# A hybrid decoder step on one core: constants of the mixing made as the norm columns arrive, the silu table loaded behind the squares, the broadcast of the first roots inside the second unit

## The chip, the core and the metric

The kernel runs on one core of a Trainium2 chip. The metric is the device time of one execution in microseconds, the median of three runs. Names of engines: PE is the matrix engine (PEld its weight loads), DVE the vector engine, ACT the scalar engine, POOL the general engine, SP the engine whose queue issues nearly all transfers.

## The reference

One layer of a decoder for 1024 prompt tokens and 8 x 8 sample tokens, all in float32, with D = 1024 and a feed-forward width of 2816:

```
x = x + 0.5 * rms_norm(swiglu(rms_norm(x, g_f1pre),  ffn1_gu, ffn1_down), g_f1post)
z = rms_norm(x, g_mix) @ w_in + b_in            # q, k, v | hq, hf, hi, hg
a = rms_norm(windowed attention with sinks(q, k, v))
f = lb + (1 - lb) * sigmoid(hf)                 # lb = first row of softmax over two rows of logits
o = rms_norm(gated recurrence(hq, f, hi)) * silu(hg)
x = x + rms_norm(concat(a, o) @ w_out, g_mixpost)
x = x + 0.5 * rms_norm(swiglu(rms_norm(x, g_f2pre), ffn2_gu, ffn2_down), g_f2post)
rms_norm(x, g) = x / sqrt(mean(x * x) + 1e-6) * g
swiglu(x, gu, down) = (silu(x @ gu[:, :2816]) * (x @ gu[:, 2816:])) @ down
```

## The kernel before

The 1088 tokens are three groups: group 0 has 256 prompt tokens and the 64 sample tokens (320 columns), groups 1 and 2 have 384 each. Every float32 product is made of three fp32r products (`mm3`, lines 258 to 260): an operand is split into a rounded high part, made by ACT (line 235 for a weight tile, 575 for the first tokens), and a remainder, made by DVE (lines 236 and 576); PE adds high x high, high x low and low x high in one bank of PSUM. Four banks of the tag `mm` go round, four of the tag `ax` serve small things.

The first feed-forward layer comes first. For group 0 it runs column block by column block of 128: a gate chain of 24 products (8 slices of D, three products each) and an up chain of 24. The first block is made in `pre_first`, where x comes in, is multiplied by the norm's gain (line 575) and used without the norm's root; the root is a factor of each token, so it is put in later, by a product with `rbs`, the roots spread over all partitions (line 664), after which come silu (665), the product with the up chain (668) and the store. To make `rbs`: ACT squares x (611), DVE adds the squares (613 to 615), PE sums over partitions (`st`, 623), DVE adds epsilon (625), POOL takes the power -1/2 (229), DVE puts the roots on a diagonal (`dg`, 630), PE multiplies it by ones (`rb`, 632), and DVE copies the result out (633).

The next blocks of group 0 are made by `up0`, with two halves of a chain between ticks; a tick lets a background stream go a step further. The stream here is the norm of group 1, then of group 2 (`pre_x` and `bcast_steps`, lines 294 to 324: squares on ACT into `ss` and `sq`, DVE's adds, `st`, `sm`, POOL's power, `dg`, `rb`), whose x is loaded by `load_x` (line 532). Weight tiles of 512 KB come over SP into three buffers (`raw`, line 242); a tile's buffer is free when DVE has made the remainder.

The order within an engine is set by a scheduler at build time, from the order of the code, its own estimates, and `issue_after`, which puts an instruction behind another one of the same engine. `queued` and `do` in `pre_first` make such chains for ACT, DVE and PE. Each engine then runs its list in order, and waits at the head of it.

The constants: `mix_consts` makes masks and, from two rows of logits in `cols`, `lb` and 1 - `lb` (with an Exp on ACT); `gains` halves two gains of norms. Both are called in the block loop of the first layer, as extra work at given blocks, but the scheduler places them.

Of the kernel before, what the change touches and what calls it, by code (L numbers as in the profile page):

```python
# [8 lines left out]
F32 = mybir.dt.float32  # L9
# [35 lines left out]
def tile_step(ctx: ExitStack, tc: tile.TileContext, A: dict, O: dict):  # L45
# [123 lines left out]
    def gains():  # L169
        V.tensor_scalar(halfpost[:, 0:8], cols[:, C_F1POST:C_F1POST + 8], 0.5, None, op0=ALU.mult)  # L170
        V.tensor_scalar(halfpost[:, 8:16], cols[:, C_F2POST:C_F2POST + 8], 0.5, None, op0=ALU.mult)

    def mix_consts():
# [41 lines left out]

        e = cp.tile([P, 3, 4], F32, name="lbe")
        l0, l1 = cols[:, C_LB:C_LB + 4], cols[:, C_LB + 4:C_LB + 8]
        V.tensor_tensor(e[:, 2], l0, l1, op=ALU.max)
        V.tensor_tensor(e[:, 0], l0, e[:, 2], op=ALU.subtract)
        V.tensor_tensor(e[:, 1], l1, e[:, 2], op=ALU.subtract)  # L220
        S.activation(e[:, 0:2], e[:, 0:2], AF.Exp)
        V.tensor_tensor(e[:, 2], e[:, 0], e[:, 1], op=ALU.add)
        V.reciprocal(e[:, 2], e[:, 2])
        V.tensor_tensor(lb, e[:, 0], e[:, 2], op=ALU.mult)
        V.tensor_scalar(omlb, lb, -1.0, 1.0, op0=ALU.mult, op1=ALU.add)

# [308 lines left out]
    def pre_first(wgu, h, wts):  # L535
# [58 lines left out]
        do("ACT", lambda: S.activation(junk[:, :P], ones, AF.Square))  # L594
# [14 lines left out]
        for hf in range(2):  # L609
            x = y[hf][:, :, :w]  # L610
            do("ACT", lambda: S.activation(x, x, AF.Square, scale=RMS))
        sq = [t[:, :, :w] for t in y]
# [18 lines left out]
        bank = axbank("rb")  # L631
        PE.matmul(bank[:, :w], ones, dg[:, :w], start=True, stop=True)
        do("DVE", lambda: V.tensor_copy(rbs, bank[:, :w]))
        return out, queued, last["PE"]
# [8 lines left out]
    def make_ffn(wgu, wdn, h, tag):  # L643
# [28 lines left out]
        def up0(j, wts, after=None):  # L672
            w = WIDTH[0]
            g, u = mmbank(), mmbank()
            for bank in (g, u):
                wt = wts.next()
                for ks in (range(4), range(4, 8)):
                    with tc.issue_after(after) if after is not None else nullcontext():
                        r = proj(bank[:, :w], wt, h[0], w, ks)
                    after = after and r.ins  # L680
                    tick()
                if bank is g:
                    rest = gated0(j, g)
            rest(u)
# [315 lines left out]
        f.begin_pair, f.pair, f.gated0 = begin_pair, pair, both0  # L1000
# [539 lines left out]
    banks, queued, tail = pre_first(A["ffn1_w_gu"], h, w0)  # L1540
    f1.rb = rbs
    with queued("ACT"), queued("DVE"):
        f1.gated0(first[0], banks)
        w0.fill()
# [33 lines left out]
    with tc.tile_pool(name="f1", bufs=1) as tp:  # L1578
        f1.pool = tp
        with tc.issue_after(f1.stored.ins):  # L1580
            xs[1] = load_x(1)
        with queued("ACT"), queued("DVE"):
            f1.up0(first[1], w0, tail)

        def norms():
            for n in (1, 2):
                yield from pre_x(n, xs[n], f1pre, part, f1)

        stream("p1", norms(), 1.1)
        for i, j in enumerate(first[2:]):  # L1590
            if i == 1:
                with tc.issue_after(f1.stored.ins):
                    xs[2] = load_x(2)
            f1.up0(j, w0)
        f1.begin(units(HEAD1))
        need("p1")
        f1.up({2: later(gains), 6: later(mix_consts), 8: misc, NJ - 1: f1.begin_down})
        f1.down(last=lambda: f1.begin_pair(PA, True))
        done1(0)
        f1.pair(PA)  # L1600
# [169 lines left out]
```

## Time and profile before

| what | value |
|---|---|
| median of three runs | 1966.09 us (1965.5 to 1967.4) |
| profiled execution: its time | 1964.23 us |
| profiled execution: its span | 1962.5 us |
| PE busy | 1944.9 us (99%) |
| DVE busy | 1368.5 us (70%) |
| ACT busy | 932.2 us (48%) |
| granted clock of PE, mean | 0.999 |

The span is from the first to the last instruction. In rows of a timeline the first number is the start in us from the span's start, the second the duration, then engine, line, operation, tiles, shape and count (xN: merged rows); a bracket at the end is the time that the engine stood idle before it, and what ended that. Matmuls are pipelined, so a row of PE is longer than its distance to the next one.

### The profile page before, as it was taken

The page shows a single profiled execution, that of the slowest core. Times are in us where ns is not written, and L with a number is a line of the kernel's source. Part 1 is how long each engine was busy: PE and PEld are TensorE (multiplying, and loading weights), DVE is VectorE, ACT ScalarE, POOL GpSimd, SP SyncE. Part 2 cuts the span into 40 slices and gives each one's busy share as a digit, 9 for nine tenths or more (in the row PEclk, how much of TensorE's full clock was granted, in tenths as well). Part 3 has the DMA queues.
Part 4 walks back from the last instruction along what each step waited for, and adds up shares of the span by engine and source line. Part 5 has one row for each costly group of instructions (what it writes and reads, how often), then busy time and mean ns, then how long its engine had stood idle before and what let it go on. Part 6 is the DMA issues. An engine that isn't in the chain of part 4 may idle for free.

```text
span 1962.5 us, 34190 instructions
## 1 busy us (share of the span) xinstructions
PE 1944.9 (99%) x13469; PEld 1828.4 (93%) x13469; DVE 1368.5 (70%) x2211; ACT 932.2 (48%) x1630; POOL 209.1 (11%) x213
## 2 busy tenths in 40 slices
PE   9999999999999999999999999999999999999998
PEld 8999999999998987788899898999999999999887
DVE  6976667777558666866667666745987877655666
ACT  6543333444455544744444565655544444444453
POOL 0000000000004012111232224001000000000202
PEclk9999999999999999999999999999999999999999
DMA  7543345556767645764434343556565545677874
GB/s 238 164 151 145 128 170 172 188 185 216 243 215 229 186 130 174 229 207 130 142 116 152 97 126 105 171 167 199 165 208 192 211 171 192 212 236 227 306 262 142
DMA packets 160396, 358.20 MB, mean 183 GB/s; under 512 B 16284, under 2 KB 59996, under 8 KB 160220
## 3 DMA queue, kind: packets, MB, share of 16 engines
q1 hardware_dynamic: 159228, 354.19, 54.5%
q8 instruction: 105, 1.72, 0.4%
q10 hardware_dynamic: 1008, 1.84, 0.3%
q14 instruction: 55, 0.45, 0.1%
HBM read 279.33 MB, written 77.63 MB: 182 GB/s over the span
## 4 chain that ended last, share of the span: by engine, by line
PE 94%; DVE 2%; DMA 2%; ACT 1%; issue 1%; POOL 0%; SPq 0%; DVEq 0%; POOLq 0%; ACTq 0%
PE mm L258 28%; PE mm L260 28%; PE mm L259 28%; DMA ar<-fa 1%; PE c L260 1%; PE c L258 1%; PE c L259 1%; PE sc L1154 1%; PE pv L1195 1%; PE lv L1228 1%; PE pT L1180 1%; DVE w L236 0%; PE mm L551 0%; PE av L1329 0%; DMA big<-in_x1T_dram 0%
## 5 line engine op out<-in xcount | busy, mean ns | idle before, releaser
L258 PE MATMUL mm<-h,wsph 128*128 128x320 f32 (+1 forms) x1296 | 416.3, 322 | 2.6 <-DVE sg L664 2.6
L259 PE MATMUL mm<-h,wsph 128*128 128x320 f32 (+1 forms) x1296 | 410.3, 317 | 0.0
L260 PE MATMUL mm<-h,wspl 128*128 128x320 f32 (+1 forms) x1296 | 408.9, 317 | 0.0
L236 DVE TENSOR_TENSOR wspl<-raw,wsph 128x1024 fp32r<-128x1024 f32 x200 | 250.7, 1254 | 148.9 <-ACT wsph L235 143.6
L235 ACT CAST wsph<-raw 128x1024 fp32r<-128x1024 f32 x200 | 208.9, 1047 | 296.0 <-PE mm L259 239.8
L235 ACT CAST w<-raw 128x512 fp32r<-128x512 f32 (+1 forms) x226 | 169.5, 754 | 239.7 <-PE mm L259 112.6
L236 DVE TENSOR_TENSOR w<-raw,w 128x512 fp32r<-128x512 f32 (+1 forms) x226 | 196.9, 875 | 85.4 <-ACT w L235 85.3
L258 PEld LDWEIGHTS mm<-h,wsph 128*128 128x128 f32 x1296 | 243.8, 188 | 10.2 <-issue 7.8
L259 PEld LDWEIGHTS mm<-h,wsph 128*128 128x128 f32 x1296 | 244.0, 188 | 1.7 <-issue 0.8
L260 PEld LDWEIGHTS mm<-h,wspl 128*128 128x128 f32 x1296 | 243.6, 188 | 1.4 <-issue 1.0
L258 PE MATMUL mm<-h,w 128*128 128x384 f32 x704 | 235.6, 335 | 0.0
L259 PE MATMUL mm<-h,w 128*128 128x384 f32 x704 | 235.6, 335 | 0.0
L260 PE MATMUL mm<-h,w 128*128 128x384 f32 x704 | 230.6, 335 | 0.0
L258 PE MATMUL mm<-w,h 128*128 128x512 f32 x462 | 181.5, 396 | 1.8 <-DVE big L940 1.3
L259 PE MATMUL mm<-w,h 128*128 128x512 f32 x462 | 180.3, 391 | 0.0
L260 PE MATMUL mm<-w,h 128*128 128x512 f32 x462 | 178.9, 391 | 0.4 <-DVE h L236 0.4
L229 POOL TENSOR_TENSOR sm<-sm,mhalf 128x3 f32<-128x3 f32 (+4 forms) x37 | 36.4, 987 | 1193.5 <-DVE sm L313 501.7
L258 PEld LDWEIGHTS mm<-h,w 128*128 128x128 f32 x704 | 132.2, 188 | 0.2 <-ACT big L754 0.2
L259 PEld LDWEIGHTS mm<-h,w 128*128 128x128 f32 x704 | 132.1, 188 | 0.0
L260 PEld LDWEIGHTS mm<-h,w 128*128 128x128 f32 x704 | 131.7, 188 | 0.0
L235 ACT CAST w<-t 128x512 fp32r<-128x512 f32 x176 | 106.8, 621 | 49.2 <-PE mm L260 46.0
L236 DVE TENSOR_TENSOR w<-t,w 128x512 fp32r<-128x512 f32 x176 | 119.0, 687 | 10.4 <-ACT w L235 10.4
(343 smaller groups left out, 3691.6 us busy)
## 6 DMA issues: line engine op xcount, KB each, us to landing
raw<-in_ffn_w_gu_dram SPq DMA_DIRECT2D x154, 512.0 KB
raw<-in_ffn_w_down_dram SPq DMA_DIRECT2D x74, 512.0 KB
raw<-in_w_in_dram SPq DMA_DIRECT2D x54, 512.0 KB
ar<-fa SPq DMA_DIRECT2D x70, 384.0 KB
big<-in_ffn_w_down_dram SPq DMA_DIRECT2D x88, 256.0 KB
fb<-big SPq DMA_DIRECT2D x44, 512.0 KB
raw<-fb SPq DMA_DIRECT2D x40, 512.0 KB
fa<-big SPq DMA_DIRECT2D x22, 768.0 KB
```

The lines of the kernel that those rows point to most:

```text
L229: G.tensor_tensor(y, x, mhalf[:y.shape[0], :y.shape[1]], op=ALU.pow)
L235: S.copy(hi, src)
L236: return (lo_eng or V).tensor_tensor(lo, src, hi.bitcast(F32), op=ALU.subtract)
L258: PE.matmul(out, a[0], b[0], start=first, stop=False, skip_group_check=resume)
L259: PE.matmul(out, a[0], b[1], start=False, stop=False, skip_group_check=resume)
L260: return PE.matmul(out, a[1], b[0], start=False, stop=last, skip_group_check=resume)
L1154: PE.matmul(banks[g][:, i * 256:i * 256 + wk], zq[64 * g:64 * g + 64, 2 * pr + i, b * P:(b + 1) * P], kx[64 * g:64 * g + 64, k0:k0 + wk], ...
L1180: PE.transpose(bank[:, (i * nk + kb) * P:(i * nk + kb + 1) * P], pt[g][:, i, kb * P:(kb + 1) * P], ident)
L1195: PE.matmul(ob[q0:q0 + 64, c:c + 64], pT[g][:, k1:k1 + 64], vn[:, vb, g * 64:g * 64 + 64], start=kb == 0, stop=kb == nk - 1)
L1228: PE.matmul(b4[ps_, j, a], x[:, a, cs], y[:, a, cs], start=True, stop=True)
```

## The change

Four things are edited. The halved gains and `lb`, `omlb` are made at the start of `pre_first`, in place of a Square on ones that had only loaded a table; the subtractions of the maximum are one instruction instead of two. Behind the two squares of x stands a Silu on ones. The matmul `rb` of the first roots, its copy to `rbs` and the gating of block A are put into a function `spread`, which `up0` calls in block B before the last slice of the up chain; block B's own gating follows its up chain. And `load_x(1)` is called after block B, no longer held behind the store of block A.

```diff
--- before.py
+++ after.py
@@ -166,10 +166,6 @@
     lb = cp.tile([P, 4], F32, name="lb")
     omlb = cp.tile([P, 4], F32, name="omlb")
 
-    def gains():
-        V.tensor_scalar(halfpost[:, 0:8], cols[:, C_F1POST:C_F1POST + 8], 0.5, None, op0=ALU.mult)
-        V.tensor_scalar(halfpost[:, 8:16], cols[:, C_F2POST:C_F2POST + 8], 0.5, None, op0=ALU.mult)
-
     def mix_consts():
         nc.sync.dma_start(sinkb, A["attn_sinks"].partition_broadcast(P))
         snk = cp.tile([4, 2], F32, name="snk")
@@ -212,18 +208,6 @@
         bank = axbank()
         PE.matmul(bank[:, 0:2], tf[:4, 7], snk, start=True, stop=True)
         V.tensor_copy(ssink, bank[:, 0:2])
-
-        e = cp.tile([P, 3, 4], F32, name="lbe")
-        l0, l1 = cols[:, C_LB:C_LB + 4], cols[:, C_LB + 4:C_LB + 8]
-        V.tensor_tensor(e[:, 2], l0, l1, op=ALU.max)
-        V.tensor_tensor(e[:, 0], l0, e[:, 2], op=ALU.subtract)
-        V.tensor_tensor(e[:, 1], l1, e[:, 2], op=ALU.subtract)
-        S.activation(e[:, 0:2], e[:, 0:2], AF.Exp)
-        V.tensor_tensor(e[:, 2], e[:, 0], e[:, 1], op=ALU.add)
-        V.reciprocal(e[:, 2], e[:, 2])
-        V.tensor_tensor(lb, e[:, 0], e[:, 2], op=ALU.mult)
-        V.tensor_scalar(omlb, lb, -1.0, 1.0, op0=ALU.mult, op1=ALU.add)
-
 
     def root(y, x):
         G.tensor_tensor(y, x, mhalf[:y.shape[0], :y.shape[1]], op=ALU.pow)
@@ -591,7 +575,18 @@
             evict(d + 2), evict(d + 3)
             weight(1, hf)
 
-        do("ACT", lambda: S.activation(junk[:, :P], ones, AF.Square))
+        e = cp.tile([P, 3, 4], F32, name="lbe")
+        l0, l1 = cols[:, C_LB:C_LB + 4], cols[:, C_LB + 4:C_LB + 8]
+        do("DVE", lambda: V.tensor_tensor(e[:, 2], l0, l1, op=ALU.max))
+        do("DVE", lambda: V.tensor_tensor(e[:, 0:2], cols[:, C_LB:C_LB + 8].rearrange("p (i a) -> p i a", i=2),
+                                          e[:, 2].unsqueeze(1).to_broadcast([P, 2, 4]), op=ALU.subtract))
+        do("ACT", lambda: S.activation(e[:, 0:2], e[:, 0:2], AF.Exp))
+        for i, c in ((0, C_F1POST), (1, C_F2POST)):
+            do("DVE", lambda: V.tensor_scalar(halfpost[:, 8 * i:8 * i + 8], cols[:, c:c + 8], 0.5, None, op0=ALU.mult))
+        do("DVE", lambda: V.tensor_tensor(e[:, 2], e[:, 0], e[:, 1], op=ALU.add))
+        do("DVE", lambda: V.reciprocal(e[:, 2], e[:, 2]))
+        do("DVE", lambda: V.tensor_tensor(lb, e[:, 0], e[:, 2], op=ALU.mult))
+        do("DVE", lambda: V.tensor_scalar(omlb, lb, -1.0, 1.0, op0=ALU.mult, op1=ALU.add))
         busy(WARM)
         operands(0)
         for i in range(2):
@@ -609,6 +604,7 @@
         for hf in range(2):
             x = y[hf][:, :, :w]
             do("ACT", lambda: S.activation(x, x, AF.Square, scale=RMS))
+        do("ACT", lambda: S.activation(junk[:, :P], ones, AF.Silu))
         sq = [t[:, :, :w] for t in y]
         do("DVE", lambda: V.tensor_tensor(sq[0], sq[0], sq[1], op=ALU.add))
         do("DVE", lambda: V.tensor_tensor(sq[0][:, :2], sq[0][:, :2], sq[0][:, 2:], op=ALU.add))
@@ -628,10 +624,18 @@
         for i in range(3):
             r = rows_of(0, i)
             do("DVE", lambda: V.tensor_scalar(dg[:, i * P:i * P + r], ident[:, :r], sm[:, 1, i:i + 1], None, op0=ALU.mult))
-        bank = axbank("rb")
-        PE.matmul(bank[:, :w], ones, dg[:, :w], start=True, stop=True)
-        do("DVE", lambda: V.tensor_copy(rbs, bank[:, :w]))
-        return out, queued, last["PE"]
+
+        def spread(after):
+            bank = axbank("rb")
+            with tc.issue_after(after):
+                r = PE.matmul(bank[:, :w], ones, dg[:, :w], start=True, stop=True)
+            do("DVE", lambda: V.tensor_copy(rbs, bank[:, :w]))
+            f1.rb = rbs
+            with queued("ACT"), queued("DVE"):
+                f1.gated0(first[0], out[0])(out[1])
+            return r.ins
+
+        return queued, spread, last["PE"]
 
     CHAIN = {1: ("X", True, False), 6: ("X", False, False), 7: ("X", False, False), 4: ("X", False, True),
              5: ("Y", True, False), 3: ("Y", False, True), 2: ("Z", True, True)}
@@ -669,18 +673,23 @@
                 f.stored = nc.sync.dma_start(acts[:, j], t[:, :w])
             return rest
 
-        def up0(j, wts, after=None):
+        def up0(j, wts, after=None, mid=None):
             w = WIDTH[0]
             g, u = mmbank(), mmbank()
             for bank in (g, u):
                 wt = wts.next()
-                for ks in (range(4), range(4, 8)):
+                parts = (range(4), range(4, 8)) if mid is None or bank is g else (range(4), range(4, 7), range(7, 8))
+                for ks in parts:
                     with tc.issue_after(after) if after is not None else nullcontext():
                         r = proj(bank[:, :w], wt, h[0], w, ks)
                     after = after and r.ins
+                    if len(ks) == 3:
+                        after = mid(after)
                     tick()
-                if bank is g:
+                if bank is g and mid is None:
                     rest = gated0(j, g)
+            if mid is not None:
+                rest = gated0(j, g)
             rest(u)
 
         def both0(j, banks):
@@ -997,7 +1006,7 @@
 
         f.head = head
         f.loads0, f.up0, f.begin, f.up, f.begin_down, f.down = loads0, up0, begin, up, begin_down, down
-        f.begin_pair, f.pair, f.gated0 = begin_pair, pair, both0
+        f.begin_pair, f.pair, f.gated0 = begin_pair, pair, gated0
         return f
 
 
@@ -1537,10 +1546,8 @@
     w0 = f1.loads0(first)
     del w0.loads[:2]
     part = {}
-    banks, queued, tail = pre_first(A["ffn1_w_gu"], h, w0)
-    f1.rb = rbs
+    queued, spread, tail = pre_first(A["ffn1_w_gu"], h, w0)
     with queued("ACT"), queued("DVE"):
-        f1.gated0(first[0], banks)
         w0.fill()
     xs = {}
 
@@ -1577,10 +1584,9 @@
 
     with tc.tile_pool(name="f1", bufs=1) as tp:
         f1.pool = tp
-        with tc.issue_after(f1.stored.ins):
-            xs[1] = load_x(1)
         with queued("ACT"), queued("DVE"):
-            f1.up0(first[1], w0, tail)
+            f1.up0(first[1], w0, tail, spread)
+        xs[1] = load_x(1)
 
         def norms():
             for n in (1, 2):
@@ -1594,7 +1600,7 @@
             f1.up0(j, w0)
         f1.begin(units(HEAD1))
         need("p1")
-        f1.up({2: later(gains), 6: later(mix_consts), 8: misc, NJ - 1: f1.begin_down})
+        f1.up({6: later(mix_consts), 8: misc, NJ - 1: f1.begin_down})
         f1.down(last=lambda: f1.begin_pair(PA, True))
         done1(0)
         f1.pair(PA)
```

What the scheduler makes of it follows, at the places that matter. Numbers behind tile names tell instances apart and differ between the two kernels; lines of the kernel after are about 16 lower than those of before for the same code, 4 higher inside `up0` and its gating.

DVE in the first microseconds behind the diagonal of the first roots. Before, from the gains to the next remainder (`sg_255` and `sg_307` are blocks A and B, `mm_125` and `mm_126` block A's gate and up banks; the copy to `rbs` and one `wspl` stand just ahead):

```order
L170 TENSOR_SCALAR halfpost<-cols 128x8
L171 TENSOR_SCALAR halfpost<-cols 128x8
L179 MEMSET amask 128x256
L218 TENSOR_TENSOR lbe<-cols 128x4
L664 TENSOR_TENSOR sg_255<-mm_125,rbs 128x320
L664 TENSOR_TENSOR sg_307<-mm_275,rbs 128x320
L236 TENSOR_TENSOR wspl_280<-raw_277,wsph_279 128x1024
L219 TENSOR_TENSOR lbe<-cols,lbe 128x4
L220 TENSOR_TENSOR lbe<-cols,lbe 128x4
L236 TENSOR_TENSOR wspl_313<-raw_310,wsph_312 128x1024
L668 TENSOR_TENSOR sg_255<-sg_255,mm_126 128x320
L668 TENSOR_TENSOR sg_307<-sg_307,mm_276 128x320
```

And in the change, from the second remainder behind the diagonal on (`sg_333` is block A):

```order
L220 TENSOR_TENSOR wspl_276<-raw_273,wsph_275 128x1024
L632 COPY rbs<-rb_330 128x320
L175 MEMSET amask 128x256
L220 TENSOR_TENSOR wspl_306<-raw_303,wsph_305 128x1024
L668 TENSOR_TENSOR sg_333<-mm_125,rbs 128x320
L668 TENSOR_TENSOR sg_341<-mm_271,rbs 128x320
L282 TENSOR_TENSOR ss_372<-ss_372,sq_374 128x384
L282 TENSOR_TENSOR ss_372<-ss_372,sq_377 128x384
L282 TENSOR_TENSOR ss_372<-ss_372,sq_380 128x384
L220 TENSOR_TENSOR wspl_357<-raw_354,wsph_356 128x1024
L282 TENSOR_TENSOR ss_372<-ss_372,sq_395 128x384
L672 TENSOR_TENSOR sg_333<-sg_333,mm_126 128x320
```

The copy, which stood directly behind the diagonal, now has two remainders ahead of it; a third stands ahead of the first gating, and four adds of the next norm and a remainder ahead of block A's second product.

SP at the start. Before:

```order
L242 DMA raw_260<-in_ffn_w_gu_dram 128x1024
L174 DMA sinkb<-in_attn_sinks_dram 128x8
L176 DMA snk<-in_attn_sinks_dram 4x2x1
L242 DMA raw_277<-in_ffn_w_gu_dram 128x1024
L242 DMA raw_310<-in_ffn_w_gu_dram 128x1024
L242 DMA raw_344<-in_ffn_w_gu_dram 128x1024
L242 DMA raw_397<-in_ffn_w_gu_dram 128x1024
L242 DMA raw_451<-in_ffn_w_gu_dram 128x1024
L669 DMA act_100<-sg_255 128x320
L532 DMA big_269<-in_x1T_dram 128x768 x2
L532 DMA big_270<-in_x1T_dram 128x768 x2
```

And in the change:

```order
L226 DMA raw_262<-in_ffn_w_gu_dram 128x1024
L516 DMA big_346<-in_x1T_dram 128x768 x2
L516 DMA big_347<-in_x1T_dram 128x768 x2
L170 DMA sinkb<-in_attn_sinks_dram 128x8
L172 DMA snk<-in_attn_sinks_dram 4x2x1
L226 DMA raw_273<-in_ffn_w_gu_dram 128x1024
L226 DMA raw_303<-in_ffn_w_gu_dram 128x1024
L226 DMA raw_354<-in_ffn_w_gu_dram 128x1024
```

The four loads of x of group 1 moved from behind the store of block A to the place right behind the third weight tile. On ACT their squares moved ahead with them: six stand in a row behind the cast of `raw_303`, then the cast of `raw_354`, then block A's silu.

PE at the norm of group 2. Before, at the end of an up chain (`mm_776`):

```order
L259 MATMUL mm_776<-h_124,wsph_695 128x320
L260 MATMUL mm_776<-h_122,wspl_696 128x320
L310 MATMUL st_711<-omean,ss_633 128x1 x3
L324 MATMUL rb_755<-dg_718,ones 128x384
L258 MATMUL mm_853<-h_121,wsph_739 128x320
```

In the change, one chain earlier (`mm_785` is that block's gate chain, `mm_786` its up chain; `rb` keeps its place behind the up chain, 26 products after these rows):

```order
L242 MATMUL mm_785<-h_122,wsph_659 128x320
L294 MATMUL st_721<-omean,ss_643 128x1 x3
L243 MATMUL mm_785<-h_124,wsph_659 128x320
L244 MATMUL mm_785<-h_122,wspl_660 128x320
L242 MATMUL mm_786<-h_121,wsph_705 128x320
```

The sums, which stood directly ahead of the broadcast that needs their roots, stand 26 products ahead of it. In the norm of group 1 the sums now stand in block D's gate chain behind 16 products, and the broadcast 33 products later. From some 800 of PE's 10,636 rows on, the order is that of before.

## The prediction

> **What bounds the kernel now.** The page's chain of waits comes first, then the waits of PE over the whole run, then the first 75 us of each engine's timeline, since the scheduled order differs only early in the program.
>
> ```profile
> PE 94%; DVE 2%; DMA 2%; ACT 1%; issue 1%; POOL 0%; SPq 0%; DVEq 0%; POOLq 0%; ACTq 0%
> ```
>
> The kernel ends when PE has done its products; another engine counts only where PE stands still. PE's own timeline has three such places in the stretch that the change touches (a bracket is the idle time just before the row, with what ended it):
>
> ```profile
> 23.34 0.70 PE L632 MATMUL rb<-dg,ones 128*128 128x320 f32 x2
> 26.67 0.38 PE L258 MATMUL mm<-h,wsph 128*128 128x320 f32 x1 [2.64 <-DVE sg L664]
> ...
> 30.27 0.31 PE L258 MATMUL mm<-h,wsph 128*128 128x320 f32 x1
> ...
> 45.39 0.83 PE L310 MATMUL st<-omean,ss 128*128 128x1 f32 x6 [0.90 <-DVE ss L298]
> ...
> 74.58 0.91 PE L324 MATMUL rb<-dg,ones 128*128 128x384 f32 x2 [2.27 <-DVE dg L320]
> ```
>
> I call the column blocks A (made in pre_first), B (the first call of up0), C and D. At 26.67 block C's gate chain needs the bank that holds block A's gate sums, and DVE frees it only by the product with the roots (sg, L664). At 30.27 block C's second chain starts without a wait. At 45.39 and 74.58 PE waits for the sums and the roots of the two other norms. Together that is 2.64 + 0.90 + 2.27 = 5.81 us: nearly all that the change can win.
>
> **The first stall: it stays.** DVE's rows of before give the lengths:
>
> ```profile
> 21.38 0.65 DVE L630 TENSOR_SCALAR dg<-ident,sm 128x128 f32<-128x128 f32 x3 [1.05 <-POOL sm L229]
> 24.07 0.49 DVE L633 COPY rbs<-rb 128x320 f32<-128x320 f32 x1 [2.04 <-PE rb L632]
> 24.48 1.22 DVE L236 TENSOR_TENSOR wspl<-raw,wsph 128x1024 fp32r<-128x1024 f32 x1
> ...
> 25.84 0.27 DVE L179 MEMSET amask<- 128x256 f32 x1
> 26.03 0.10 DVE L218 TENSOR_TENSOR lbe<-cols 128x4 f32<-128x4 f32 x1
> 26.05 0.88 DVE L664 TENSOR_TENSOR sg<-mm,rbs 128x320 f32<-128x320 f32 x2
> 26.84 1.29 DVE L236 TENSOR_TENSOR wspl<-raw,wsph 128x1024 fp32r<-128x1024 f32 x1
> ...
> 28.20 1.21 DVE L236 TENSOR_TENSOR wspl<-raw,wsph 128x1024 fp32r<-128x1024 f32 x1
> 29.34 0.87 DVE L668 TENSOR_TENSOR sg<-sg,mm 128x320 f32<-128x320 f32 x2
> ...
> 40.65 1.21 DVE L298 TENSOR_TENSOR ss<-ss,sq 128x384 f32<-128x384 f32 x2
> ...
> 73.85 0.67 DVE L320 TENSOR_SCALAR dg<-ident,sm 128x128 f32<-128x128 f32 x3
> 74.44 0.88 DVE L664 TENSOR_TENSOR sg<-mm,rbs 128x320 f32<-128x320 f32 x2
> ```
>
> The rb matmul now stands three products earlier, at (30.27 - 26.67) / 24 = 0.15 us each (a chain has 24) 0.45 us. Its copy could start at 24.07 - 0.45 = 23.62. But the order of DVE now has two weight remainders (wspl) between dg and that copy, and a third ahead of sg, where before one stood ahead of sg. Distances between starts: three dg 0.59 (73.85 to 74.44), a wspl 1.14 (28.20 to 29.34), the copy 0.41 (24.07 to 24.48), the memset 0.19 (25.84 to 26.03), a sg pair 0.79 (26.05 to 26.84), and from the start of sg to PE's resumption 0.62 (26.05 to 26.67). So: 21.38 + 0.59 + 2 x 1.14 = 24.25 for the copy, + 0.41 + 0.19 + 1.14 = 25.99 for sg, + 0.62 = 26.61 for PE. That is 0.06 us earlier than 26.67. What the two halfpost gains and the lbe steps gave up on DVE, the extra remainders take back.
>
> **The third remainder and a new wait.** Are its inputs there? ACT's timeline:
>
> ```profile
> 4.07 1.28 ACT L594 ACT_TABLE_LOAD   x1 [4.07 <-DMA cols<-in_cols_dram]
> ...
> 14.34 1.27 ACT L611 ACTIVATE big<-big 128x1280 f32<-128x1280 f32 x1
> 15.52 1.99 ACT L235 CAST wsph<-raw 128x1024 fp32r<-128x1024 f32 x2
> 19.28 1.05 ACT L235 CAST wsph<-raw 128x1024 fp32r<-128x1024 f32 x1 [1.78 <-DMA raw<-in_ffn_w_gu_dram]
> 23.23 1.04 ACT L235 CAST wsph<-raw 128x1024 fp32r<-128x1024 f32 x1 [2.90 <-DMA raw<-in_ffn_w_gu_dram]
> 24.29 1.28 ACT L665 ACT_TABLE_LOAD   x1
> 26.56 0.87 ACT L665 ACTIVATE sg<-sg 128x320 f32<-128x320 f32 x2 [0.99 <-DVE sg L664]
> 27.45 1.28 ACT L221 ACT_TABLE_LOAD   x1
> 28.74 0.21 ACT L221 ACTIVATE lbe<-lbe 128x8 f32<-128x8 f32 x1
> ...
> 36.56 1.57 ACT L297 ACTIVATE sq<-big 128x384 f32<-128x384 f32 x3
> ```
>
> The fifth weight tile lands at 23.23 and its cast ends at 24.27, before 24.25 + 0.60 = 24.85, where DVE wants it: 0.58 us of slack. Behind sg DVE now does three ss adds (the next norm's squares, because its input is loaded earlier), a wspl, an ss add, and only then the second product of block A (sg times mm, L668 of before), which frees the bank of block C's second chain. 25.99 + 0.79 = 26.78; three adds at 0.60 (half of 1.21) make 28.58; the wspl 29.72; one add 30.32; + 0.62 gives PE at 30.94. PE arrives at 26.61 + 3.60 = 30.21. So a wait of **0.73 us** opens where there was none. On ACT the six squares take at most 24.27 + 6 x 0.52 = 27.4, and the cast behind them ends at 28.4, 0.2 us ahead of DVE's need at 28.58. Its tile can be issued when the third remainder ends (21.97 + 1.22 = 23.19) and lands some 3.5 us later (15.72 to 19.28 in the rows below): 26.7, in time. Bounds of the new wait: 0 if the adds run on without gaps and the arrival slips, 1.7 if that tile lands a microsecond later than so reckoned.
>
> **The input of the second token group, moved ahead on SP.**
>
> ```profile
> 8.31 0.43 SPq L174 DMA_DIRECT2D sinkb<-in_attn_sinks_dram  x1
> ...
> 15.72 14.05 SPq L242 DMA_DIRECT2D raw<-in_ffn_w_gu_dram  x5
> 29.84 0.41 SPq L669 DMA_DIRECT2D act<-sg  x1
> 30.30 2.31 SPq L532 DMA_DIRECT2D big<-in_x1T_dram  x4
> ```
> ```profile
> GB/s 265 259 337 345 390 365 369 366 372 367 395 385 399 408 420 423 420 437 417 432 387 417 432 417 387 417 417 359 286 141 76 2 0 0 60 0 0 0 0 0
> ```
>
> The second fence is the transfer rate over 5 to 16 us in 40 slices of 0.275 us: about 400 GB/s until 12.7 us, then nothing. The four x1T loads (4 x 384 KB = 1.57 MB, 3.9 us at 0.4 MB/us) now stand right behind the first three weight tiles, so they fall into that hole: 12.7 + 3.9 = 16.6. They are moved past the sink loads, which nothing early reads, and past six weight tiles. The fourth tile leaves at 15.72, when a raw buffer is freed, and its bytes come after the hole's end or share its last 0.9 us; its remainder has slack (cast ended 20.3, DVE wants it at 23.11). I take nothing for it; the bound is in the rivals.
>
> **The two norm waits: they go.** With x1T issued some 21 us sooner (30.30 before, about 9 now), the st matmuls stand in block D's gate chain after 16 products (they stood a block later). PE is there at 30.94 + 3.60 + 16 x 0.15 = 36.9. DVE's last ss add comes after the second products (30.32 + 0.79), two adds, a sg, a wspl and that add: 31.11 + 1.2 + 0.4 + 1.14 + 0.6 = 34.45, and the cast that this wspl needs is done by 31.3 (PE has read the weights that it overwrites at 30.2, + 1.05). That leaves over 2 us, so the 0.90 goes. The rb of that norm is 33 products later, 4.85 us, against this chain:
>
> ```profile
> 46.62 1.89 POOL L229 TENSOR_TENSOR sm<-sm,mhalf 128x3 f32<-128x3 f32 x1 [19.57 <-DVE sm L313]
> 72.34 0.16 DVE L313 TENSOR_SCALAR sm<-st 128x3 f32<-128x3 f32 x1 [1.78 <-PE st L310]
> 72.58 0.85 POOL L229 TENSOR_TENSOR sm<-sm,mhalf 128x3 f32<-128x3 f32 x1 [24.07 <-DVE sm L307]
> ```
>
> From st to the end of dg takes the 2.27 us that PE waited at 74.58, or 2.27 + 1.04 = 3.3 with the slow power of 1.89. In the second norm st and rb stood next to each other; now 26 products, 3.8 us, lie between them. That covers 3.3, so the 2.27 goes too.
>
> **The start and the table loads.** Exp takes the place of the first Square behind the same load at 4.07, so no load is added there. Its operands need cols, which had landed by 4.07; DVE's five following small steps at 0.2 each:
>
> ```profile
> 6.58 1.01 DVE L576 SCALAR_TENSOR_TENSOR h<-big,cols,h 128x320 fp32r<-128x320 f32 x2 [5.49 <-ACT h L575]
> 31.63 0.17 DVE L223 RECIPROCAL lbe<-lbe 128x4 f32<-128x4 f32 x1
> 31.83 0.16 DVE L224 TENSOR_TENSOR lb<-lbe 128x4 f32<-128x4 f32 x1
> ```
>
> Exp ends near 4.07 + 1.30 + 0.21 = 5.58, four dependent steps at 0.20 end at 6.4, and DVE idles until 6.58: hidden, at worst 0.2 us if not. The silu load goes behind the squares: ACT 14.34 + 1.27 = 15.61, + 1.28 + 0.31 = 17.2, then the cast of block B's second weight ends at 18.2 instead of 16.5. PE's order puts that chain at 19.1 by count of products, and its remainder starts only after the squares' sums, at 18.44 before; 0.2 us of slack. The loads at 24.29, 27.45 and the one after them cost PE nothing before (their idle neighbours wait for DVE and DMA), so dropping them wins nothing. [...]
>
> Behind 75 us I see no new stall: where DVE is full,
>
> ```profile
> 80.00:100.00 20.00, 20.00 (x139) 20.00 (x138) 20.00 (x18) 13.19 (x14) 0.00 (x0) 1.00 0.36 103
> ```
>
> (PE, PEld, DVE and ACT busy, in that order) PE was full as well, and DVE's chain starts from the same rb matmul, so both move forward together. If that cover failed, up to the gain itself would be given back.
>
> **Sum** against the profiled execution (span 1962.5, time 1964.23): - 0.06 + 0.73 - 0.90 - 2.27 = **-2.5**, so 1960.0 and 1961.7. The median of the three runs is 1966.09, 1.9 above the profiled one; carried over: 1966.1 - 2.5 = **1963.6**. The likeliest case's own range takes the new wait from 0 to 1.7: 1962.9 to 1964.6, and a microsecond of spread between medians on either side.
>
> **Rivals.**
> 1. *The waits only move.* DVE is late with the ss adds too, and the norm waits stay: -0.06 + 0.73 = +0.7, 1966.8. For it: DVE gains a wspl ahead of every step of this part. Against: the 2 us of slack. 0.14.
> 2. *More goes than counted.* The new wait stays away and the first stall shrinks by 0.7 or more, up to all of it: -3.9 to -5.9, 1962.2 to 1960.2. For it: the first stall is what the moved broadcast stands before. Against: the two remainders ahead of the copy. 0.13.
> 3. *Slower: x1T takes transfer time from the weights.* Place: 8.3 to 16.6 us on the DMA engines. If all of its 3.9 us falls on the fifth tile, sg comes 3.9 - 0.6 = 3.3 later and PE with it: -2.5 + 3.3 = +0.8, 1966.9; if it falls on the first operands, which ACT takes without idle time, 3.9 more: 1970.8. It decides from a delay of 0.58 + 2.5 = 3.1 us on. Against: the rate is at its top until 12.7 whether x1T is queued or not, and the fifth tile's transfer is after 19.66. 0.10. [...]
> [...]
>
> **How the numbers follow.** The forecast has 0.59. A measurement of this kernel tells 0.2%, 3.9 us, from no change. Faster by more than that needs rival 2 (0.13); slower by more needs the upper half of rival 3 and a bad sum in rival 1 (0.08); the rest, 0.79, is within. The range reaches down to nearly all of rival 2, 1960.4, and up through rival 1 to the lower end of rival 3, 1967.0.
>
> **What would show it.** Right: PE's wait near 26.6 for sg is still 2.3 to 2.8 us; a new wait of 0.3 to 1.7 near 30.2 for the second product of block A; no PE wait at either st or rb; x1T issued from 8.3 on and done before 17; no table load between 20 and 45 us. Wrong: a first wait under 2 us (rival 2), tiles four and five landing after 19.5 and 23.5 (rival 3), a cast of block B's second weight after 18.5 (rival 4), st or rb still waited for (rival 1).

## The result and the profile after

| what | before | after |
|---|---|---|
| median of 11 runs each | 1965.0 us (1962.82 to 1967.4) | 1960.77 us (1958.28 to 1963.14) |
| ratio after / before, 95% interval | | 0.9978 (0.997 to 0.9985) |
| profiled execution: time, span | 1964.23, 1962.5 us | 1958.28, 1956.2 us |
| PE busy | 1944.9 us | 1942.2 us |

The kernel is 4.2 us faster, which is 0.22% (interval 0.15 to 0.30%): just over the 0.2% that the prediction reckoned a measurement to tell from no change. The time lies inside the predicted range of 1960.4 to 1967.0, 2.8 us under the predicted 1963.6. (1.1 us of that is the base: the three runs of before that the prediction had stood at 1966.09, the eleven at 1965.0.) The profiled execution of the kernel after is the fastest of its eleven.

PE's waits in the profile after, the largest first (waited for in us, times, longest):

```profile
PE mm L242 <- DVE sg L668: 2.6, 1, 2.6
PE kT L1333 <- DVE h L424: 1.7, 1, 1.7
PE mm L242 <- DVE big L949: 1.3, 2, 0.9
```

The waits of 2.3 us at `rb` and of 0.9 us at `st` are no longer in the list; the first stall heads it as before. PE's own timeline after, at the four places of the prediction:

```profile
26.52 0.38 PE L242 MATMUL mm<-h,wsph 128*128 128x320 f32 x1 [2.56 <-DVE sg L668]
...
30.11 0.31 PE L242 MATMUL mm<-h,wsph 128*128 128x320 f32 x1
...
35.83 0.31 PE L242 MATMUL mm<-h,wsph 128*128 128x320 f32 x1
35.98 0.72 PE L294 MATMUL st<-omean,ss 128*128 128x1 f32 x6
...
36.80 0.31 PE L244 MATMUL mm<-h,wspl 128*128 128x320 f32 x1
...
66.33 0.72 PE L294 MATMUL st<-omean,ss 128*128 128x1 f32 x6
...
70.81 0.81 PE L308 MATMUL rb<-dg,ones 128*128 128x384 f32 x2
...
71.60 0.31 PE L243 MATMUL mm<-h,wsph 128*128 128x320 f32 x1
```

The same places before, as far as the prediction has not shown them:

```profile
44.18 0.31 PE L259 MATMUL mm<-h,wsph 128*128 128x320 f32 x1
...
46.31 0.31 PE L258 MATMUL mm<-h,wsph 128*128 128x320 f32 x1
...
71.58 0.72 PE L310 MATMUL st<-omean,ss 128*128 128x1 f32 x6
...
75.07 0.56 PE L258 MATMUL mm<-h,wsph 128*128 128x320 f32 x1
75.47 0.31 PE L259 MATMUL mm<-h,wsph 128*128 128x320 f32 x1
```

The second product behind the second norm's `rb` is a good mark, since the same products lie ahead of it in both (290 from the end of the first stall on): it starts at 75.47 before and at 71.60 after, **3.87 us earlier**. The pieces:

- first stall: 26.67 to 26.52, -0.15;
- the sums of norm 1, from the product ahead of them to the second one behind: 44.18 to 46.31 is 2.13 us before; 35.83 to 36.80 is 0.97 us after: -1.16;
- norm 2: from `st` to the mark 3.89 us before (71.58 to 75.47); after 5.27 us (66.33 to 71.60), but with 26 products of 0.147 us in between, so 1.45: -2.44;
- these make -3.75; the rest, -0.12, is a hiccup of about 0.1 us near 40.7 us in before.

Two of the three large waits are gone, and the third stayed at its size. The profiled spans differ by 6.3 us, more than these 3.87 and more than the medians' 4.2. Much of the rest is one stretch. Windows of before and then of after (columns: us, then busy time and count of PE, PEld, DVE, ACT, POOL; then granted clock, DMA share, GB/s):

```profile
900.00:910.00 10.00, 10.00 (x62) 7.41 (x62) 4.78 (x9) 3.44 (x3) 0.00 (x0) 0.83 0.34 108
```
```profile
900.00:910.00 10.00, 10.00 (x90) 8.67 (x89) 7.55 (x16) 7.88 (x9) 2.53 (x2) 1.00 0.49 141
```

In before the granted clock is 0.83 there against 1.00 after, worth about 1.7 us (an estimate: 10 us x 0.17). It is no property of before: a later profile of the unchanged new kernel has 0.88 in that window.

```profile
900.00:910.00 10.00, 10.00 (x82) 8.66 (x82) 6.15 (x12) 5.64 (x5) 2.01 (x2) 0.88 0.53 156
```

### The profile page after: what moved, and what is told of

Same layout as the page of the kernel before. It is cut to its first block, busy times and chain, and to the rows that moved or that the text cites. A ratio compares the mean times of both kernels' runs of the same rounds, so it can differ in the third digit from the quotient of the medians.

```text
span 1956.2 us, 34187 instructions
## 1 busy us (share of the span) xinstructions
PE 1942.2 (99%) x13469; PEld 1826.3 (93%) x13469; DVE 1368.3 (70%) x2210; ACT 930.1 (48%) x1628; POOL 208.1 (11%) x213
## 4 chain that ended last, share of the span: by engine, by line
PE 95%; DMA 2%; DVE 2%; ACT 1%; issue 0%; POOL 0%; SPq 0%; DVEq 0%; POOLq 0%; ACTq 0%
PE mm L242 28%; PE mm L244 28%; PE mm L243 28%; DMA ar<-fa 1%; PE c L244 1%; PE c L242 1%; PE c L243 1%; PE sc L1163 1%; PE pv L1204 1%; PE lv L1237 1%; PE pT L1189 1%; DVE w L220 0%; PE av L1338 0%; PE su L1460 0%; PE av L1341 0%
```

## The experiments

The times are medians beside a kernel before of 1965.1 or 1965.0 us. "The mark" is the second product behind the second norm's `rb`: 75.47 before, 71.60 after. (The expectations call it the first product behind; their numbers are for this row.) In the diffs `...` marks lines left out.

**The early load alone**, on the kernel before:

```diff
-        with tc.issue_after(f1.stored.ins):
-            xs[1] = load_x(1)
         with queued("ACT"), queued("DVE"):
             f1.up0(first[1], w0, tail)
+        xs[1] = load_x(1)
```

> The kernel before with one edit: the loads of x of group 1 called after block B and no longer held. In its order the sums of the first norm stand 34 products ahead of their broadcast (before: 26), those of the second norm 6 products ahead (before: 0, in the change 26). Theory (the early load is what the change won by, the moved broadcast won nothing at the first stall): PE's wait of 0.90 at the first st goes and costs 1.2 less, the wait at the second rb shrinks from 2.27 by 6 x 0.15 = 0.9 to about 1.4, the first stall stays at 2.6; PE's first product behind the second rb at 75.5 - 2.1 = 73.4 us, time about 2 us under before. Rival (the broadcast inside block B is what made room): 75.2 to 75.7 us and no change.

Measured: 1961.49 us, ratio 0.9982 (0.9973 to 0.9992). PE:

```profile
26.52 0.61 PE L258 MATMUL mm<-h,wsph 128*128 128x320 f32 x1 [2.64 <-DVE sg L664]
26.92 0.47 PE L259 MATMUL mm<-h,wsph 128*128 128x320 f32 x1
...
41.25 0.72 PE L310 MATMUL st<-omean,ss 128*128 128x1 f32 x6
...
73.48 0.91 PE L324 MATMUL rb<-dg,ones 128*128 128x384 f32 x2 [1.05 <-DVE dg L320]
```

The wait at the first `st` is gone, that at the second `rb` is down from 2.27 to 1.05, and the mark comes at 74.38 instead of the expected 73.4. What is lost there is not a wait: behind the first stall, products start 0.27 us apart instead of 0.147, some eleven times, which costs about 1.4 us. That half clock (granted 0.50 over 26.5 to 29.7 us) is taken up below; without it the mark would be near 73.0. So one edit of the four has some 2.5 of the 3.9 us at the mark, and 3.6 of the 4.2 us of the medians (about 2 was expected; the interval spans 1.6 to 5.3 us).

**The changed kernel with that load held back** behind the store of block A:

```diff
...
-        xs[1] = load_x(1)
+        with tc.issue_after(f1.stored_a.ins):
+            xs[1] = load_x(1)
```

> The changed kernel with one edit: the loads of x of group 1 held behind the store of block A, as before. In its order st and rb of the second norm stand next to each other again. Theory: both norm waits are back (about 0.9 and 2.3), the first stall is 2.5 to 2.6, PE's first product behind the second rb at 75.2 to 75.4, time within 0.5 us of before. Rival: at least 2 of the 3.9 us stay, 73.5 or earlier.

Measured: 1966.53 us, ratio 1.001 (1.0 to 1.0019); that is 1.4 us above before, where at most 0.5 was expected. The waits are back, the one at `st` at half its size:

```profile
43.89 0.83 PE L294 MATMUL st<-omean,ss 128*128 128x1 f32 x6 [0.41 <-DVE ss L282]
...
73.82 1.65 PE L308 MATMUL rb<-dg,ones 128*128 128x384 f32 x2 [2.27 <-DVE dg L304]
...
75.53 0.47 PE L243 MATMUL mm<-h,wsph 128*128 128x320 f32 x1
```

The mark is at 75.53, as in before (expected 75.2 to 75.4). Part of that is half clock (granted 0.55 over 74.5 to 77 us): from `rb` to the mark it takes 1.71 us here and 0.89 in before. At full clock the mark would be near 74.7, so without the early load the three other edits win at most 0.8 us in the trace, and nothing in the median.

**The constants alone**, on the kernel before: `gains` and the `lbe` steps moved to the start of `pre_first`, as in the change.

> The kernel before with only the constants (halved gains, lb, omlb) made at the start in place of the Square. Theory: DVE's gating of block A comes 0.25 earlier, first stall 2.4, both norm waits as before (0.9 and 2.3), PE's first product behind the second rb at 75.1 to 75.4, time within 0.5 us of before. Rival (the constants made the room for the gain): 73.5 or earlier.

Measured: 1965.99 us, ratio 1.0002 (0.9993 to 1.0011), no change; first stall 2.43, the `rb` wait 2.27 at 74.58, the mark at 75.48. The three small steps that DVE no longer makes ahead of the first gating (two gains, the first of `lbe`) shorten the stall by 0.2 us, and nothing of it is left later. (Behind the stall 13 products ran at half clock, granted 0.51 over 27.8 to 31.2, some 1.5 us; PE came to the first `st` so much later that no wait is left there, and the mark stayed.)

**The Silu on ones left out** of the changed kernel:

```diff
-            do("ACT", lambda: S.activation(junk[:, :P], ones, AF.Silu))
```

> The changed kernel without the Silu on ones; the table load then stands ahead of block A's silu, 1.28 us on ACT at about 27.9. Theory (that load has cover: DVE comes to block A's second product at 30.1 only, and no PE wait hangs on it): PE's first product behind the second rb at 71.5 to 71.8, time as the change. Rival (the early load is worth its 1.28): 72.7 or later.

Measured: 1961.39 us, ratio 0.9981 (0.9972 to 0.999). ACT then loads the table in front of block A's silu:

```profile
28.10 1.28 ACT L668 ACT_TABLE_LOAD   x1
29.39 0.83 ACT L668 ACTIVATE sg<-sg 128x320 f32<-128x320 f32 x2
```

PE's first wait is again 2.56, no wait appears at `st` or `rb`, and the mark is at 73.25, of which some 1.45 us is the half clock again, granted 0.52 over 26.6 to 29.9 (the expected 71.5 to 71.8 holds without it). Where the table is loaded costs PE nothing that shows.

**The broadcast back in its old place**, right behind block A, in the changed kernel:

```diff
     queued, spread, tail = pre_first(A["ffn1_w_gu"], h, w0)
+    spread(tail)
...
-            f1.up0(first[1], w0, tail, spread)
+            f1.up0(first[1], w0, tail)
```

> The changed kernel with one edit: matmul, copy and gating of the first roots called right behind block A's program, as before; constants, silu load and early x load stay. In its order st of the second norm stands 7 products ahead of rb. Theory: first stall 2.4 to 2.7, no wait at the first norm's st, 1.3 left at the second rb, PE's first product behind it at 72.9 to 73.3, time 2.4 us under before. Rival (the moved broadcast shortens the first stall): the wait grows to 3.0 or more.

Measured: 1961.25 us, ratio 0.9984 (0.9974 to 0.9993). PE:

```profile
26.59 0.39 PE L242 MATMUL mm<-h,wsph 128*128 128x320 f32 x1 [2.43 <-DVE sg L668]
...
71.96 0.91 PE L308 MATMUL rb<-dg,ones 128*128 128x384 f32 x2 [0.91 <-DVE dg L304]
```

The first stall is no longer than with the broadcast moved (2.43 against 2.56), so the move does nothing for the wait that it stands before. What returns is 0.9 us of the wait at the second `rb` (1.3 was expected). In the scheduled order `st` of norm 2 stands 7 rows ahead of `rb` here, 6 in the kernel with the early load alone, and 27 in the changed kernel. So the move of the broadcast acts 45 us later, through the places that the scheduler then finds for the background stream. The mark is at 72.85, 1.25 later than after; the medians (1961.25 and 1960.77) do not resolve that. Together with the 2.5 us of the early load this accounts for the 3.9 us at the mark within 0.2.

**The gating first**: weights fetched one ahead during block B, the rest issued behind block A's gating, so that one remainder instead of two lies between `dg` and the copy to `rbs`, and none between the copy and the gating.

(`gate_a` is that gating.)

```diff
...
+        w0.n = 1
         with queued("ACT"), queued("DVE"):
             f1.up0(first[1], w0, tail, spread)
+        w0.n = 3
+        with tc.issue_after(f1.gate_a.ins):
+            w0.fill()
         xs[1] = load_x(1)
```

> The changed kernel with one edit: no weight tile beyond the third is split until block A's gating is issued, so one remainder instead of two stands ahead of the copy of the roots and none between copy and gating. Theory (the two remainders hold the first stall): copy at 23.6, gating at 24.2, PE's wait for it about 0.7 instead of 2.56. The second norm's st stands 3 products ahead of rb here (26 in the change), so about 1.9 of its wait comes back: PE's first product behind the second rb near 71.6, time as the change. Rival (the roots' matmul or the bank sets the stall): the wait stays at 2.3 or more.

Measured: 1960.91 us, ratio 0.9977 (0.9968 to 0.9987). DVE and PE:

```profile
21.66 0.65 DVE L626 TENSOR_SCALAR dg<-ident,sm 128x128 f32<-128x128 f32 x3 [1.05 <-POOL sm L213]
22.22 1.22 DVE L220 TENSOR_TENSOR wspl<-raw,wsph 128x1024 fp32r<-128x1024 f32 x1
23.91 0.49 DVE L632 COPY rbs<-rb 128x320 f32<-128x320 f32 x1 [0.47 <-PE rb L631]
...
24.59 0.82 DVE L669 TENSOR_TENSOR sg<-mm,rbs 128x320 f32<-128x320 f32 x2
```
```profile
25.16 0.38 PE L242 MATMUL mm<-h,wsph 128*128 128x320 f32 x1 [0.86 <-DVE sg L669]
...
71.11 0.91 PE L308 MATMUL rb<-dg,ones 128*128 128x384 f32 x2 [1.49 <-DVE dg L304]
...
72.01 0.30 PE L243 MATMUL mm<-h,wsph 128*128 128x320 f32 x1
```

The first stall falls from 2.56 to 0.86 us: the remainders ahead of copy and gating held it, as the prediction had it. (Now the copy waits 0.47 us for the matmul `rb`.) But the order has moved again: `st` of norm 2 now stands 3 rows ahead of `rb`, a wait of 1.49 opens there, and of 1.7 us nothing is left at the mark (72.01 against 71.60).

**The second product of block A made late**, in the changed kernel: a fill and eight dependent reciprocals on a spare tile between its gating and that product.

```diff
...
-                f1.gated0(first[0], out[0])(out[1])
+                rest = f1.gated0(first[0], out[0])
+            last["DVE"] = f1.gate.ins
+            do("DVE", lambda: V.memset(dly, 1.0))
+            for _ in range(8):
+                do("DVE", lambda: V.reciprocal(dly, dly))
+            with queued("DVE"):
+                rest(out[1])
...
```

> The changed kernel with nine tiny DVE steps (a fill, then eight reciprocals of 16 elements, each waiting for the one before) put between block A's gating and its second product; they work on a spare tile and change no result. In the order the second product now stands behind block C's gating, so it ends after 33 us. Theory (block C's up chain does not use block A's up bank, because the bank that was freed first is given next): that chain starts 3.6 us after its gate chain without a wait. Rival (the banks go round in turn, as the prediction assumed): it waits 2.5 us or more for the second product.

Measured: 1960.74 us in a single run. DVE's row of block A's second product, and a window (PE's busy time is the second number):

```profile
33.79 0.43 DVE L679 TENSOR_TENSOR sg<-sg,mm 128x320 f32<-128x320 f32 x1
```
```profile
29.60:38.00 8.40, 8.40 (x59) 8.40 (x59) 6.90 (x16) 2.89 (x4) 0.99 (x2) 1.00 0.61 188
```

Block C's up chain starts at 31.35 (its gate chain at 26.31, half of it at half clock, granted 0.51 over 26.4 to 29.6), 2.4 us before that product, and PE is busy without a break until 38. So this product does not free the bank of that chain. In the changed kernel it cannot be block B's up bank either: both second products start from 30.09 on, one behind the other, and the chain at 30.11. Of the four `mm` banks that leaves the two gate banks: the pair of gatings at 25.90 had freed both, so block C's gate chain can take the one and its up chain the other.

**The gating first, and norm 2's broadcast later**: the same edit as in the kernel with the gating first, and two more steps of the background stream between `dg` and `rb`.

```diff
         yield
         yield
+        for _ in range(more):
+            yield
         rb = axbank("rb")
...
-        yield from bcast_steps(cell, 384, rb)
+        yield from bcast_steps(cell, 384, rb, more=2)
...
```

> The kernel that gates block A first (no tile beyond the third split before it), and in the norms of groups 1 and 2 the broadcast two ticks later, so that st of the second norm stands 34 products ahead of rb. Theory (the two gains add up once st and rb are apart): first stall 0.7 to 0.9, no wait at st or rb of either norm, PE's first product behind rb of the second norm (which stands 36 products later here) at 70.4 + 5.3 = 75.7, time 1.3 to 1.7 us under the change. Rival (DVE has no room left, so the wait turns up at another place behind it): time as the change or more.

Measured, in five runs: **1958.18 us, ratio 0.9962 (0.9948 to 0.9975)**, 6.8 us under before. PE:

```profile
25.29 0.39 PE L242 MATMUL mm<-h,wsph 128*128 128x320 f32 x1 [0.86 <-DVE sg L671]
...
69.35 0.72 PE L294 MATMUL st<-omean,ss 128*128 128x1 f32 x6
...
74.86 0.81 PE L310 MATMUL rb<-dg,ones 128*128 128x384 f32 x2
...
75.65 0.31 PE L243 MATMUL mm<-h,wsph 128*128 128x320 f32 x1
```

`rb` has moved 36 products further down, so its mark at 75.65 answers to 75.65 - 36 x 0.147 = 70.4 in the order of after: 1.2 earlier than after, 5.1 earlier than before. No wait is left at either norm. It is faster than before beyond its interval. Its median lies 2.6 us under that of after (1.3 to 1.7 was expected), but the two were not timed beside each other, and their ratios to before (0.9948 to 0.9975 and 0.997 to 0.9985) overlap a little; the 1.2 us at the mark is what the trace shows.

**The unchanged kernels once more**, one profile and one run each, to see how far the half clock belongs to a kernel.

> The changed kernel, unaltered, once more, to see whether the clock after its first stall is always full. If the half clock behind a wait of TensorE of over 2.3 us is a matter of chance in each execution, some of the repeats show 11 to 13 products of block C at about 0.27 us each behind the first stall (its wait again 2.4 to 2.7 us), and the first product behind the second roots is then near 73.0 us instead of 71.6. If it is a property of the kernels that showed it, this one shows products of about 0.147 us there and 71.6 again.

> The kernel before, unaltered, once more. If the half clock is a matter of chance, the stretch behind its first stall (wait 2.5 to 2.7 us) may show it, with the first product behind the second roots near 76.9 us; if it belongs to other kernels only, that product starts near 75.5 us as in the first profile.

> As the second profile of the changed kernel: 71.6 us for the first product behind the second roots where the clock stays full behind the first stall, about 73.0 us where some 12 products run at half clock.

> The kernel with the gating first and the second roots' broadcast later, unaltered, once more. Its waits of TensorE up to 60 us are 0.9 us at most, so the half clock should not appear whichever account holds: products of block C at about 0.147 us behind the first stall, and the first product behind the second roots at 75.6 to 75.8 us in its own place.

Measured: the changed kernel 1959.11 and 1960.54 us, the first stall 2.56 in both, at full clock (1.00 over 25 to 80 us), the mark at 71.77 and 71.61. The kernel before 1964.42 us, the first stall 2.64 at full clock (1.00 over 25 to 30.2 us), but then half clock behind the wait at `rb` (0.50 over 76.3 to 79.6), with the mark at 75.93 ahead of it. The kernel with both edits 1957.45 us, stall 0.86, no half clock (1.00 over 25 to 80 us), its mark at 75.17 instead of the expected 75.6 to 75.8, because its first stall ended 0.48 sooner (24.81 against 25.29). The first profile of the changed kernel is thus typical up to the mark, within 0.2 us. That of before is 0.46 us early (its repeat has one wait more, of 0.36 us at 41.47), so the gain at the mark is 3.7 to 4.3 us over all pairs of profiles. The half clock also comes to an unchanged kernel.

## Why the prediction was right, and where it was wrong

**The first stall: right.** Predicted 26.61 for PE, -0.06; measured 26.52, -0.15. (The repeats have 26.69 and 26.53 after and 26.80 before, so a difference of 0.1 us is within their scatter.) DVE after:

```profile
21.32 0.65 DVE L626 TENSOR_SCALAR dg<-ident,sm 128x128 f32<-128x128 f32 x3 [1.05 <-POOL sm L213]
21.88 2.35 DVE L220 TENSOR_TENSOR wspl<-raw,wsph 128x1024 fp32r<-128x1024 f32 x2
24.15 0.48 DVE L632 COPY rbs<-rb 128x320 f32<-128x320 f32 x1
...
25.90 0.87 DVE L668 TENSOR_TENSOR sg<-mm,rbs 128x320 f32<-128x320 f32 x2
30.09 0.88 DVE L672 TENSOR_TENSOR sg<-sg,mm 128x320 f32<-128x320 f32 x2
```

The copy was predicted at 24.25 (it came at 24.15), the gating at 25.99 (25.90), the second product at 30.32 (30.09). The kernel with the gating first showed the reason too: with one remainder ahead, the stall is 0.86.

**The third remainder and a new wait: wrong. This is the step that failed.** The work on DVE came out as laid out, but the wait of 0.73 did not open: block C's up chain started at 30.11 without a wait, while the product that was to free its bank started only at 30.09. The prediction had taken block A's up bank for that chain. The delayed product showed that it is another: the chain ran although that product started 2.4 us behind it. The bounds of this term (0 to 1.7) held the value; the value taken was not 0, and the four banks had not been followed one by one to what frees each.

**The two norm waits: right in kind, undersized.** Counted as 0.90 + 2.27 = 3.17, measured as 1.16 + 2.44 = 3.60. The idle time in brackets is not all that a stop costs: the row of `rb` behind its wait in before runs 0.91 long, and without a wait 0.81, and from `rb` to the mark it takes 0.89 instead of 0.79. That both waits would go held. So did the room for it, about: DVE's last add of norm 1 ends at 34.10 and PE comes to `st` at 35.98; the last `dg` of norm 2 ends at 68.89 and `rb` is at 70.81, 1.9 us each, where over 2 and 0.5 to 1.5 had been reckoned. The cause is the early load, as the single edit and its removal showed; the broadcast's move adds its share at the second `rb` through the order, which the prediction had read from that order.

**The loads.** SP and ACT after:

```profile
8.23 2.48 SPq L516 DMA_DIRECT2D big<-in_x1T_dram  x4
```
```profile
14.27 1.27 ACT L606 ACTIVATE big<-big 128x1280 f32<-128x1280 f32 x1
15.56 1.28 ACT L607 ACT_TABLE_LOAD   x1
16.85 0.31 ACT L607 ACTIVATE junk<-ones 128x128 bf16<-128x128 f32 x1
...
20.45 1.05 ACT L219 CAST wsph<-raw 128x1024 fp32r<-128x1024 f32 x1 [1.40 <-DMA raw<-in_ffn_w_gu_dram]
```

The x1T loads went out from 8.23, as said, and the DMA rate over 5 to 18 us stays near 400 GB/s until 16.4 (40 slices of 0.325 us) instead of 12.7:

```profile
GB/s 329 342 374 347 363 333 326 364 399 406 393 396 386 440 442 416 403 403 429 403 429 416 416 403 394 419 381 416 416 388 407 397 397 416 397 328 310 210 225 362
```

No table load stands between 20 and 45 us, as predicted. Rival 3 had part of its mechanism: the fourth tile's cast started at 20.45 instead of 19.28, 1.17 us later, past the 19.5 set as its sign. Both casts stood waiting for their tile's transfer (1.78 us before, 1.40 after); that the early load costs the 1.17 us is the author's estimate. The tile's remainder was not wanted until 23.11 (by the prediction), so this cost nothing; the fifth tile's cast came at 23.19, as before. The 0.04 of the chances beside the three rivals stood for a table load that costs more than its own 1.28 us, with a cast of block B's second weight after 18.5 as its sign. No run shows such a cost: the square ahead ends at 15.54, the load starts at 15.56, takes 1.28, the next row starts at 16.85, and that cast starts at 17.07. The kernel without the Silu says the same (28.10 + 1.28 = 29.38, silu at 29.39).

**The sum.** Against the predicted -2.5: the new wait's 0.73 not paid, 0.43 more from the norms, 0.09 more at the first stall, 0.12 from the hiccup, which makes -3.87, the mark's distance. The medians differ by 4.2. **The chances.** "Within 0.2%" had 0.79, and the result stands a hair outside, at 0.22%. The range held the time only by the part drawn for rival 2: the likeliest case's own, 1962.9 to 1964.6 with a microsecond on either side, ends 1.1 us above it. Rival 2 (0.13) has the result in its price, 1962.2 to 1960.2, but only half of its mechanism: the new wait stayed away, the first stall did not shrink. That the time came out inside the range is thus in part luck. With -2.5 as the likeliest and a bound at -3.9, the bounds of the new wait alone (down to 0, so -3.2) and any undersizing of the norms led to the line; 0.13 was too little for that.

## What to carry to other kernels

When a wait is foreseen because "that product frees the bank", follow each bank of the pool by name, from the instruction that frees it to the chain that takes it, before the wait gets a price. Where a stream is placed by a scheduler, look for the effect of an edit where the order changes, and not only where the code was edited: here 0.9 us was won 45 us behind the moved line, and a shortening of 1.7 us was given back by 3 rows between `st` and `rb` until those two were moved apart as well. Price a wait of the matrix engine by the distance between the products around it; the idle time shown was the lower end at both waits here (0.90 against 1.16, 2.27 against 2.44).

## What was not expected of the hardware

Behind waits of PE of 2.3 to 2.6 us, the products that follow run at half clock (granted 0.50 to 0.55 in windows of 2.5 to 3.4 us) for about 3 us in some executions, and at full clock in others. Windows behind the first stall in before, with the early load alone, and (both stalls) with the constants alone; last, behind the second `rb` in the repeat of before:

```profile
26.60:29.80 3.20, 3.13 (x21) 3.16 (x22) 3.20 (x7) 2.72 (x5) 0.40 (x1) 1.00 0.68 182
```
```profile
26.50:29.70 3.20, 3.18 (x12) 3.20 (x13) 3.20 (x7) 2.04 (x5) 0.40 (x1) 0.50 0.71 191
```
```profile
27.80:31.20 3.40, 3.40 (x15) 3.40 (x14) 2.88 (x5) 1.04 (x1) 0.00 (x0) 0.51 0.63 211
75.60:79.00 3.40, 3.40 (x15) 3.40 (x14) 3.40 (x8) 0.23 (x1) 0.00 (x0) 0.51 0.56 207
```
```profile
76.30:79.60 3.30, 3.30 (x14) 3.30 (x13) 3.30 (x8) 0.00 (x0) 0.00 (x0) 0.50 0.34 133
```

PE is busy nearly throughout in all of them; only the granted clock (the third number from the end) and the count of products differ, 12 instead of 21 in the same time. Eleven to thirteen products, each 0.12 us longer, cost some 1.4 us, and no list of waits shows it. (With the load held back the slow stretch took in the `rb` rows and six products.) Over all profiles, from 23 to 80 us: of fifteen waits of 2.27 to 2.64 us seven were followed by it, of ten waits of 0.36 to 1.49 us none. The unchanged kernel before has it in one of its two profiles and not in the other, so it is a matter of the execution; the kernel with both edits, whose longest wait there is 0.86, shows it in neither of its two profiles up to 80 us. That may be why the kernel with both edits gains 6.8 us where its waits account for 5.1; that this is the reason was not shown.

A wait of 2.3 us is not what it takes, though. The stretch near 900 us is the same thing without any wait in the trace: in before, behind four products `su` with operands on 32 partitions (the first at 899.71), with PE busy throughout, the clock is 0.50 over 902.9 to 906.3 us, and products start 0.32 us apart there instead of 0.174. Of five profiles (before, after and their repeats) two show a lower clock there: before with 0.83 over 900 to 910, the third of after with 0.95 over 890 to 900 and 0.88 over 900 to 910; the other three have 1.00. And near 820 us before and after have a wait of 1.67 us at a transpose (`kT`), with the clock at 1.00 from 800 to 840. What brings it about near 900 no run settles.

Nor does the length of a wait tell: of the four waits of 2.27 us three were followed by half clock (the load held back, the constants alone, the repeat of before) and one, in before, was not (1.00 over 75.6 to 78.9). How long PE has to stand idle for it no run here settles.
